# A macaron block with conv and gated linear attention: x by chunks at the head, the mixer's weights and its end in a new order

## The chip, the cores and the metric

One core of a Trainium2 chip runs one launch of the kernel. Its engines each work through a list of their own: TensorE (PE, with PEld for its weight loads), VectorE (DVE), ScalarE (ACT), GpSimd (POOL) and SyncE (SP), which here only issues transfers. The metric is the device time of the launch in microseconds (us), the median of the runs shown.

## The reference, cut to what matters

The input x has 512 rows of 1024 numbers (float32), and there is one layer:

```python
h = h + 1/2 * SwiGLU_1(RMSNorm(h))             # FFN1: 1024 -> 2 x 2816 -> 1024
u = RMSNorm(h); z = u @ W_in                   # mixer: conv value and gate, q, k, v, r, forget gate
y_conv = silu(LayerNorm(depthwise_conv31(GLU)))
y_gla  = rmsnorm_per_head(chunked gated linear attention) * silu(r)
h = h + concat([y_conv, y_gla]) @ W_out
h = h + 1/2 * SwiGLU_2(RMSNorm(h))             # FFN2
h = h + sigmoid(RMSNorm(h) @ W_g) * (p @ W_p)
out = RMSNorm(h)

def _swiglu(x, w_in, w_out):
    gate, up = jnp.split(x @ w_in, 2, axis=-1)
    return (jax.nn.silu(gate) * up) @ w_out
```

The norm of a row is a factor on that row, so a product can be started on x times the norm's gains, and the row's factor put on its result.

## The kernel before, in words

**Data and products.** Everything is kept transposed: features on the 128 partitions, the 512 rows along the free axis, so x is turned by TensorE (a product with the identity, `ident`) in eight chunks of 128 features, each with four 128x128 turns into one PSUM bank. Each factor of a product is cut in a high part of fewer bits (a cast, on ACT as a rule) and a low part, what the cast left (a subtraction, on DVE). A product of 128 features is then three matmuls of 512 columns: `mm3` does high by high, high weight by low x, low weight by high x. For x the parts are `hgH` and `hgL`; for weights `wr` is the raw tile, `wh` and `wl` its parts of 128x1024 (six of each), and `wa` parts of 128x512 in smaller buffers. There are two ways to make `wl`: the subtraction on DVE or POOL (`low`), or `added`, where ACT writes minus the rounded weight to it and a transfer issued by POOL adds the raw weight to that.

**The FFNs** use a scheme with fewer products: for most pairs of 256 of the 2816 features, seven products (units `m1` to `m7`) of half the rows (256 columns) on sums of weight and x blocks; the first two pairs, and those listed as `plain`, are computed plainly (units `h0` to `h7`). A list of units sets the order; before a unit runs, the parts of later units are prepared: a unit names jobs with a distance, and `AHEAD` is 4, so the cast of a unit's weights is put on ACT and DVE four units ahead (lines 580 to 600, 715 to 740). `hooks` puts other work after a named unit. The output product is done in parts over pairs (`second`, pieces named by their output column n and half g).

**The head** (lines 140 to 557) loads x in pieces by rows: four of 128x256 twice, and four of 128x512, and the weights of the first four output blocks between them (two gate, two up blocks of 128 features). The first two, `pg0` and `pu0`, use 128x4x128 pieces; `pg1` and `pu1` come after, each over all eight chunks of x (`zblock`). In the last of these, at chunk 7, `spread` puts the rows' norm factors over the partitions (four transposes). Squares of x, from which the norm comes, are summed by ACT, twelve instructions with an accumulator. SP issues the transfers in the order of the program.

**The end of FFN1 and the mixer.** `ahead` prepares the first weights of the mixer, four raw tiles of `in_w_in` with eight `wa` pairs, all from the hook of unit `m4` of pair 10. POOL makes their low parts. In the mixer, z's blocks for tokens (`tokblock`, four times, t = 0 to 3) are followed each by the gate `r` (ACT), the tokens' `y` times `r` (DVE, `y<-y,r`), and some of the convolution's taps (`taps(n)`, DVE instructions `cv<-glu,cw,cv`). Then TensorE turns `y`, ACT and DVE cut it in `ygH` and `ygL`, and the output product starts (`first_part(n)`, 12 matmuls for output block n on the attention's half, with weights `wo[n]`). The conv's LayerNorm runs beside it: `mub` collects the mean by products with the constant `mean` on the four conv blocks (the last two as one sum, `acc23`), `ln_sums` the squares, `ln_out` spreads the factor, and `yc` are the conv's outputs. These are put between matmuls of `first_part(3)` and `first_part(6)`.

Of the kernel before, what the change touches and what calls it, by code (L numbers as in the profile page):

```python
# [15 lines left out]
P = 128  # L16
# [46 lines left out]
def block_kernel(ctx: ExitStack, tc: tile.TileContext, a: dict, out: bass.AP):  # L63
# [75 lines left out]
    in_order(True)  # L139
    columns(vecs[:1], 8, "vcol1", nc.sync)()  # L140
    X_CUTS = (0, 2 * P, 4 * P, D)
    xt = [[] for _ in range(TB)]

    def load_x(i):

        c0, c1 = X_CUTS[i:i + 2]
        for t in range(TB):
            piece = bt(s="x")[:, 0:c1 - c0]
            nc.sync.dma_start(out=piece, in_=a["x"][0, t * P:(t + 1) * P, c0:c1])  # L149
            xt[t].append(piece)  # L150


# [57 lines left out]
    def parts(r3):  # L210

        return low(high(r3))
# [231 lines left out]
    hT = [big.tile([P, SEQ], F32, tag="H", bufs=DC, name=nm("h")) for _ in range(DC)]  # L444
    hg, xps = [], []

    def turn_x(c):
        ps = bank()
        for t in range(TB):
            i = min(c // 2, 2)  # L450
            c0 = c * P - X_CUTS[i]
            pe.transpose(ps[:, t * P:(t + 1) * P], xt[t][i][:, c0:c0 + P], ident)
        xps.append(ps)
# [3 lines left out]

    def take(ps, w, ks):

        for k in ks:  # L460
            mm3(ps, *rows_of(w, k), *hg[k], k == 0, k == DC - 1)

    ssx = tmp("ssx", 16, bufs=1)

    def square_x(i):
        for t in range(TB):
# [3 lines left out]
    def halves(c0):  # L470

        r3 = raw(DC, P)
        for k in range(0, DC, 4):
            def go(k=k):
                fetch(r3[:, k:k + 4], ffn1_in, k, 4, c0, P)
                return r3[:, k:k + 4]
            yield go

    def big4(r3):
        hi, lo = (bt(F32R, "wa").rearrange("p (k c) -> p k c", k=4) for _ in range(2))  # L480
        act.copy(hi, r3)
        return hi, lo, r3

    go_g, go_u = list(halves(0)), list(halves(DFF))
    load_x(0)
    raw_g = [go_g[0]()]
    load_x(1)
    raw_u = [go_u[0]()]
    raw_g.append(go_g[1]())
    load_x(2)  # L490
    raw_u.append(go_u[1]())
    turn_x(0)
    turn_x(1)
    pg0, pu0 = bank(), bank()
    split_x(0)
    wg0 = [low(big4(raw_g[0]))]
    split_x(1)
    take(pg0, wg0, (0,))
    turn_x(2)
    turn_x(3)  # L500
    split_x(2)
    take(pg0, wg0, (1,))
    split_x(3)
    wu0 = [low(big4(raw_u[0]))]
    take(pg0, wg0, (2, 3))
    act.copy(hT[0], xps[0])
    dve.tensor_copy(hT[1], xps[1])
    take(pu0, wu0, (0, 1))
    turn_x(4)
    take(pu0, wu0, (2, 3))  # L510
    wg0.append(low(big4(raw_g[1])))
    split_x(4)
    turn_x(5)
    split_x(5)
    act.copy(hT[2], xps[2])
    dve.tensor_copy(hT[3], xps[3])
    turn_x(6)
    take(pg0, wg0, (4,))
    split_x(6)
    turn_x(7)  # L520
    take(pg0, wg0, (5,))
    split_x(7)
    wu0.append(low(big4(raw_u[1])))
    raw_g1 = load(ffn1_in, 0, DC, P, P)
    raw_u1 = load(ffn1_in, 0, DC, DFF + P, P)
    take(pg0, wg0, (6, 7))
    take(pu0, wu0, range(4, DC))
    w1 = Left(ffn1_in, 2)
# [4 lines left out]
    for i in range(P // RANK):  # L533
        nc.sync.dma_start(out=made[2][i * RANK:(i + 1) * RANK, :], in_=a["gate_w_up"][0])
    square_x(0)
    early = [parts(raw_g1), parts(raw_u1)]
    for c in range(4, DC, 2):
        act.copy(hT[c], xps[c])
        dve.tensor_copy(hT[c + 1], xps[c + 1])
    square_x(1)  # L540
    square_x(2)
    ss = tmp("cs", 16)[:, :TB]
    dve.tensor_reduce(out=ss, in_=ssx.rearrange("p (t i) -> p t i", t=TB)[:, :, 0:3],
                      axis=mybir.AxisListType.X, op=ALU.add)
    mid = [rsqrt_mean(ss, D, TB, between=lambda: w1.part("a11"))]
    pg1 = zblock(early[0], hg)
    pu1 = zblock(early[1], hg, {2: lambda: w1.part("a12"), 7: lambda: mid.append(spread(mid[0]))})
    xb = Right(hg, "ffn1_norm")


# [51 lines left out]
    def ffn(w_in, w_out, x, gname, given, first, rsb, hooks, plain):  # L602
# [10 lines left out]
        def row(i):  # L613
            return rsb[:, i * HALF:(i + 1) * HALF].unsqueeze(1).to_broadcast([P, 2, HALF])

# [16 lines left out]
        def scaled(ps, name):  # L632
            o = tmp(name)
            dve.tensor_tensor(out=o, in0=ps, in1=rsb, op=ALU.mult)
            return o
# [106 lines left out]

        def second(cut):
# [53 lines left out]
            if not last:  # L797
                return [piece(n, 0, True, True, ("g2", f0) if n == 0 else None) for n in range(0, DC, 2)]
            return ([piece(n, 0, True, False) for n in range(0, 6, 2)],
                    [piece(n, 1, False, True) for n in range(0, 6, 2)] + [piece(6, 0, True, False),  # L800
# [11 lines left out]
        for i in plain:  # L812
            for j in range(8):
                add(f"h{j}", i)
                if j % 2:
# [25 lines left out]
        p0 = pairs[0]  # L841
        for i in range(2):
            s = silu(scaled(first[i][0], "g1"))
            gated_block(p0, s, scaled(first[i][1], "u1"), i)
        more = hooks.get(("h0", 1), lambda *_: None)
        hooks["h0", 1] = lambda *_: (act_parts(p0), more())
        drive(units)
# [12 lines left out]
    hooks = sums_hooks(xb, ("t2", "t3", "t1", "t4"), (("h7", 1), ("h2", 2), ("h5", 2), ("m1", 3)))  # L860
    hooks.update({("h%d" % (i + 1), 1): f for i, f in enumerate(xb.steps())})
    hooks.update({("m5", 3): lambda *_: made[0](), ("m5", 4): lambda *_: constants(),
                  ("m4", 10): lambda *_: w_ahead.extend([ahead(w_in, D_CONV, 2 * P), ahead(w_in, 0, 2 * P)])})
    rsb = mid[1]
    hg, norm = ffn(ffn1_in, a["ffn1_w_out"][0], xb, "mix_norm", {0: Left(ffn1_in, 0), 1: w1},
                   ((pg0, pu0), (pg1, pu1)), rsb, hooks, (1, 2))
    pool.on = False
# [356 lines left out]
    def part(ps, w, ks, first, last, mid={}):  # L1224
        for k in ks:
            if k in mid:
                mid[k]()
            mm3(ps, *rows_of(w, k), *mix[k], first and k == ks[0], last and k == ks[-1])

# [7 lines left out]
    for t in range(TB):  # L1237
# [20 lines left out]
        if t == 1:  # L1258
            oload(2)
            ytok = []  # L1260
            for i in range(TB):
# [18 lines left out]
    pe.matmul(mub, mean, acc[1], start=False, stop=False)  # L1280
    taps(2)
    for h in range(4):
# [58 lines left out]

    first_part(3, wo[3], {4: ln_sums})
    first_part(6, wo[6], {5: ln_out})

# [189 lines left out]
```

## Time and profile before

| | |
|---|---|
| median of 3 runs | 959.59 us (959.04 to 960.14) |
| the profiled execution | 959.53 us, its span 957.8 us |
| TensorE busy in the span | 941.6 us (98%), 5790 matmuls and turns |
| DVE, ACT, POOL busy | 732.2, 450.3 and 49.7 us |
| mean granted TensorE clock | 0.997 |

The span is the time from the first to the last recorded work; 1.73 us of the execution lie around it. Instruction names read out<-in, so `ps<-hgH,wh` is a matmul into a PSUM bank from the high parts of x and weights; all instructions carry line L46, that of a helper which records the order, so the names tell them apart. Since TensorE is busy for 98%, the question of every edit is which of its few idle times, or which slow stretch, it touches.

### The profile page before, as it was taken

The numbers are of one execution on the slowest core, as the hardware profiler recorded it, in microseconds if no ns is written. First come the engines' busy times: TensorE is split into PE (matmuls) and PEld (weight loads), VectorE is DVE, ScalarE is ACT, GpSimd is POOL, SyncE is SP. The second block draws the span as 40 slices with busy tenths as digits, with TensorE's granted clock in tenths as the row PEclk, the third lists the DMA queues.
The fourth block names the chain that finished last, engine by engine and source line by source line (L and its number), as shares of the span: only waits on it lengthen the run. The fifth ranks groups of instructions, "written<-read, shape, count | busy, mean of one in ns | idle before, by whom it ended". The sixth has DMA issues, their size and how long they took to land.

```text
span 957.8 us, 14314 instructions
## 1 busy us (share of the span) xinstructions
PE 941.6 (98%) x5790; PEld 835.6 (87%) x5790; DVE 732.2 (76%) x979; ACT 450.3 (47%) x694; POOL 49.7 (5%) x59
## 2 busy tenths in 40 slices
PE   7999999999999999999999999999999999999996
PEld 5888999999999978888878889999999999998885
DVE  4685888887788585999995749787878778867554
ACT  5753443434443463473564855444334443346442
POOL 0000200000000210101030010000000000000000
PEclk9999999999999999999999999999999999999998
DMA  7632323342323471337553571432244233334102
GB/s 223 184 111 66 97 81 108 113 133 74 104 89 110 142 188 45 88 89 175 118 112 104 153 176 44 132 110 67 91 129 121 74 102 102 111 111 154 44 1 88
DMA packets 105510, 104.49 MB, mean 109 GB/s; under 512 B 4756, under 2 KB 96582, under 8 KB 105445
## 3 DMA queue, kind: packets, MB, share of 16 engines
q1 hardware_dynamic: 102708, 94.67, 32.1%
q0 software_dynamic: 2736, 8.91, 5.3%
q8 instruction: 45, 0.74, 0.3%
q14 instruction: 21, 0.16, 0.1%
HBM read 92.56 MB, written 2.10 MB: 99 GB/s over the span
## 4 chain that ended last, share of the span: by engine, by line
PE 92%; issue 2%; DVE 2%; DMA 2%; ACT 1%; POOL 1%; SPq 0%; POOLq 0%; DVEq 0%; ACTq 0%
PE ps L46 91%; DMA wr<-in_w_in 1%; PE ax L46 1%; DVE cv L46 1%; ACT wh L46 0%; DMA wr<-in_ffn_w_in 0%; POOL rs L46 0%; DVE y L46 0%; DVE wl L46 0%; ACT wl L46 0%; ACT wa L46 0%; POOL wa L46 0%; SPq L149 0%; DVE rs L46 0%; DVE g L46 0%
## 5 line engine op out<-in xcount | busy, mean ns | idle before, releaser
L46 DVE TENSOR_TENSOR wl<-wr,wh 128x1024 fp32r<-128x1024 f32 (+1 forms) x168 | 199.7, 1201 | 47.4 <-ACT wh L46 46.9
L46 PE MATMUL ps<-hgH,wh 128*128 128x256 f32 (+1 forms) x752 | 235.3, 313 | 0.0
L46 PE MATMUL ps<-hgH,wl 128*128 128x256 f32 (+1 forms) x752 | 234.9, 312 | 0.0
L46 PE MATMUL ps<-hgL,wh 128*128 128x256 f32 (+1 forms) x752 | 234.9, 312 | 0.0
L46 ACT CAST wh<-wr 128x1024 fp32r<-128x1024 f32 (+1 forms) x183 | 185.0, 1026 | 33.8 <-PE ps L46 23.1
L46 PEld LDWEIGHTS ps<-hgL,wh 128*128 128x128 f32 x752 | 143.4, 191 | 8.8
L46 PEld LDWEIGHTS ps<-hgH,wh 128*128 128x128 f32 x752 | 143.4, 191 | 8.7
L46 PEld LDWEIGHTS ps<-hgH,wl 128*128 128x128 f32 x752 | 143.4, 191 | 8.2
L46 PE MATMUL ps<-actH,wh 128*128 128x512 f32 x352 | 137.6, 391 | 1.2 <-ACT actH L46 1.2
L46 PE MATMUL ps<-actL,wh 128*128 128x512 f32 x352 | 137.5, 391 | 0.2 <-DVE actL L46 0.2
L46 PE MATMUL ps<-actH,wl 128*128 128x512 f32 x352 | 137.0, 389 | 0.0
L46 ACT ACTIVATE s<-g 128x512 f32<-128x512 f32 x48 | 30.4, 632 | 187.6 <-DVE g L46 187.6
L46 DVE SCALAR_TENSOR_TENSOR cv<-glu,cw,cv 128x502 f32<-128x502 f32 (+24 forms) x120 | 82.1, 741 | 0.6
L46 PEld LDWEIGHTS ps<-actH,wh 128*128 128x128 f32 x352 | 66.2, 188 | 14.4 <-ACT actH L46 1.6
L46 PEld LDWEIGHTS ps<-actH,wl 128*128 128x128 f32 x352 | 66.1, 188 | 13.9
L46 PEld LDWEIGHTS ps<-actL,wh 128*128 128x128 f32 x352 | 66.2, 188 | 13.1 <-DVE actL L46 0.5
L46 DVE SCALAR_TENSOR_TENSOR h<-ps,h 128x512 f32<-128x512 f32 x80 | 54.4, 688 | 22.1 <-PE ps L46 22.1
L46 ACT COPY sq<-ps 128x512 f32<-128x512 f32 x34 | 19.9, 585 | 73.8 <-PE ps L46 73.8
L46 PE MATMUL ps<-wh,hgH 128*128 128x512 f32 (+1 forms) x136 | 52.4, 385 | 0.0
L46 PE MATMUL ps<-wl,hgH 128*128 128x512 f32 (+1 forms) x136 | 51.7, 380 | 0.0
L46 PE MATMUL ps<-wh,hgL 128*128 128x512 f32 (+1 forms) x136 | 51.3, 377 | 0.0
L46 ACT CAST actH<-m 128x512 fp32r<-128x512 f32 x44 | 25.4, 618 | 39.2 <-DVE m L46 39.2
(230 smaller groups left out, 1656.9 us busy)
## 6 DMA issues: line engine op xcount, KB each, us to landing
wr<-in_ffn_w_in SPq DMA_DIRECT2D x86, 512.0 KB
wr<-in_ffn_w_out SPq DMA_DIRECT2D x32, 512.0 KB
wr<-in_w_in SPq DMA_DIRECT2D x20, 512.0 KB
wl<-wr POOLq DMA_DIRECT2D x15, 512.0 KB, 5.0
wr<-in_ffn_w_out SPq DMA_DIRECT2D x16, 384.0 KB
wr<-in_w_out SPq DMA_DIRECT2D x8, 512.0 KB
wr<-in_ple_w_gate SPq DMA_DIRECT2D x8, 512.0 KB
out<-y SPq DMA_DIRECT2D x8, 256.0 KB
```

What stands on the lines that cost most here:

```text
L46: inst = call(*args, **kwargs)
```

## The change

The diff has four groups. The first is the **head**: the first chunk of x (all rows, 128 columns) is the first transfer of SP, the first norm's gains move to ACT's queue, x comes by column chunks and weights by rows of one or two chunks (for all four blocks), and the four blocks are accumulated together, chunk after chunk, 12 matmuls each. `warm_up` adds 14 turns of the identity whose result isn't used. Squares are whole tiles on ACT with a reduction on DVE, and `spread` and the first pairs' gates (`first_out`) move behind unit `h0`. Two steps of FFN1's block sums (`xb.steps()`) come earlier, and later ones at other units. The second is **`ahead`**: low parts by `added`, and its second call after piece n = 4 of the last output part, `("last", 4)`. The third is the distance of `m5`'s cast, `AHEAD + 1` in each pair rather than in the first alone. The fourth is the **mixer's end**: order of the three matmuls, of taps, casts and LayerNorm steps.

```diff
     in_order(True)
-    columns(vecs[:1], 8, "vcol1", nc.sync)()
-    X_CUTS = (0, 2 * P, 4 * P, D)
...
+    def warm_up(n):
+        idle = aux()
+        for _ in range(n):
+            pe.transpose(idle[:, 0:P], ident, ident)
+
+    warm_up(10)
+    turn_vec = columns(vecs[:1], 8, "vcol1", nc.scalar)
...
-        return [[low(w, pool) for w in high4(load(src, 0, DC, c, P))] for c in range(c0, c0 + ncol, P)]
+        return [[added(w) for w in high4(load(src, 0, DC, c, P))] for c in range(c0, c0 + ncol, P)]
...
+    def load_x(c, n):
+        nt = TB // n
+        for h in range(n):
+            tile_ = bt(s="x").rearrange("p (t c) -> p t c", t=nt)
+            nc.sync.dma_start(out=tile_, in_=a["x"][0, h * nt * P:(h + 1) * nt * P, c * P:(c + n) * P]
+                              .rearrange("(t p) c -> p t c", p=P))
...
     def square_x(i):
-        for t in range(TB):
-            junk = tmp("sq", bufs=3)[:, 0:X_CUTS[i + 1] - X_CUTS[i]]
-            act.activation(junk, xt[t][i], AF.Square, accum_out=ssx[:, 4 * t + i:4 * t + i + 1])
...
+        act.activation(sq, tile_, AF.Square)
...
+        dve.tensor_reduce(out=sums[-1][:, t0:t0 + nt], in_=sq, axis=mybir.AxisListType.X, op=ALU.add)
...
+    def take(k, between):
+        wh, wl = (t[:, k % 2] for t in wpart[k // 2])
+        xh, xl = hg[k]
+        for i, (w, x) in enumerate(((wh, xh), (wl, xh), (wh, xl))):
+            for b in range(4):
+                c0 = (b // 2 + 2 * (b % 2)) * P
+                pe.matmul(ps0[b], w[:, c0:c0 + P], x, start=(k == i == 0), stop=(k == DC - 1 and i == 2))
+            if i == 1:
+                between()
+
+    for c in range(2):
+        load_x(c, 1)
+        load_w(c, 1)
+    load_x(2, 2)
+    load_w(2, 1)
+    load_w(3, 1)
+    for c in (4, 6):
+        load_x(c, 2)
+        load_w(c, 2)
...
+    turn_vec()
+    turn_x(0)
+    warm_up(4)
+    ps0 = [bank() for _ in range(4)]
+    split_w(0, 1, dve.tensor_copy)
+    split_x(0)
...
+    for c in range(DC):
+        nxt = {0: (1,), 1: (2, 3), 3: (4, 5), 5: (6, 7)}.get(c, ())
+        take(c, lambda: [turn_x(n) for n in nxt])
+        if c < 3:
+            split_w(c + 1, 1)
+        elif c in (3, 5):
+            split_w(c + 1, 2)
+        for n in nxt:
+            split_x(n)
+        keep_x(c)
...
-            before = [(AHEAD + (kind == 'm5' and i == start), lambda: p.part(part))] if part else []
+            before = [(AHEAD + (kind == 'm5'), lambda: p.part(part))] if part else []
...
-                  ("m4", 10): lambda *_: w_ahead.extend([ahead(w_in, D_CONV, 2 * P), ahead(w_in, 0, 2 * P)])})
+                  ("m4", 10): lambda *_: w_ahead.append(ahead(w_in, D_CONV, 2 * P)),
+                  ("last", 4): lambda *_: w_ahead.append(ahead(w_in, 0, 2 * P))})
...
+            wo[4] = [added(w) for w in ohigh(4)]
...
-        if t > 1:
-            wo[t + 2] = [added(w) for w in ohigh(t + 2)]
+        if t == 2:
+            wo[5] = [added(w) for w in ohigh(5)]
         if t > 0:
-            taps((0, 2, 5, 5)[t])
+            taps((0, 2, 5, 2)[t])
...
-    taps(2)
+    taps(1)
...
-    pe.matmul(mub, mean, acc23, start=False, stop=True)
-    first_part(5, wo[5])
+    first_part(5, wo[5], {6: lambda: pe.matmul(mub, mean, acc23, start=False, stop=True)})
...
-    first_part(3, wo[3], {4: ln_sums})
-    first_part(6, wo[6], {5: ln_out})
+    first_part(3, wo[3], {6: ln_sums})
+    first_part(6, wo[6], {6: ln_out})
```

At **the head, on SP**, the transfers before were these (`x` four pieces of rows, `wr` weights of one block):

```order
L122 DMA vcol1r<-in_ffn_norm 8x128
L149 DMA x_98<-in_x 128x256
L149 DMA x_100<-in_x 128x256
L149 DMA x_102<-in_x 128x256
L149 DMA x_104<-in_x 128x256
L181 DMA wr_96<-in_ffn_w_in 128x4x128
L149 DMA x_107<-in_x 128x256
```

And now, with `x` all rows of one chunk, and `wr` one chunk's rows for two gate and two up blocks:

```order
L447 DMA x_108<-in_x 128x4x128
L482 DMA wr_104<-in_ffn_w_in 128x256 x2
L447 DMA x_112<-in_x 128x4x128
L482 DMA wr_104<-in_ffn_w_in 128x256 x2
L447 DMA x_116<-in_x 128x2x256
L447 DMA x_118<-in_x 128x2x256
L482 DMA wr_105<-in_ffn_w_in 128x256 x4
```

The first weights moved from the sixth transfer to the second and third. On TensorE, now, at the same place:

```order
L46 MATMUL ax_81<-ident 128x128 x10
L46 MATMUL ax_161<-ident,vcol1r 128x8
L46 MATMUL ps_164<-ident,x_108 128x128 x4
L46 MATMUL ax_169<-ident 128x128 x4
L46 MATMUL ps_174<-hgH_182,wh_178 128x512
L46 MATMUL ps_175<-hgH_182,wh_178 128x512
L46 MATMUL ps_176<-hgH_182,wh_178 128x512
L46 MATMUL ps_177<-hgH_182,wh_178 128x512
```

Four blocks (`ps_174` to `ps_177`) now take chunk 0 after four turns of x; before, eight turns stood ahead of the first block's first matmul.

At **the end of FFN1, on ACT**, before (`wa` the mixer's weights, `wh` FFN1's last output weights, `actH` the last features):

```order
L46 CAST wa_3347<-wr_3345 128x512
L46 CAST wa_3350<-wr_3345 128x512
L46 CAST wa_3357<-wr_3355 128x512
L46 CAST wa_3360<-wr_3355 128x512
L46 CAST wh_3367<-wr_3229 128x768
L46 ACTIVATE s_3397<-g_588_3395 128x512
L46 CAST wh_3399<-wr_3264 128x768
L46 CAST actH_3424<-m_3323 128x512
```

And now:

```order
L46 ACTIVATE wa_3350<-wr_3347 128x512
L46 ACTIVATE wa_3353<-wr_3347 128x512
L46 CAST wh_3361<-wr_3239 128x768
L46 ACTIVATE s_3391<-g_568_3389 128x512
L46 CAST wh_3393<-wr_3274 128x768
L46 CAST actH_3418<-m_3333 128x512
L46 CAST actH_3422<-m_3333 128x512
L46 CAST wh_3426<-wr_3300 128x768
L46 CAST wa_3452<-wr_3450 128x512
L46 CAST wa_3455<-wr_3450 128x512
```

The third and fourth raw tiles of the mixer moved behind `actH`; `ACTIVATE wa` is the negated copy of `added`.

At **the mixer's end, on DVE**, before (`y` the last token block, `ygL` the first low parts for the output product):

```order
L46 SCALAR_TENSOR_TENSOR cv_3617<-glu_4035,cw,cv_3617 128x502
L46 SCALAR_TENSOR_TENSOR cv_3617<-glu_4035,cw,cv_3617 128x503
L46 SCALAR_TENSOR_TENSOR cv_3617<-glu_4035,cw,cv_3617 128x504
L46 SCALAR_TENSOR_TENSOR cv_3617<-glu_4035,cw,cv_3617 128x505
L46 TENSOR_TENSOR y_4725<-y_4725,r_4802 128x512
L46 SCALAR_TENSOR_TENSOR cv_3617<-glu_4035,cw,cv_3617 128x506
L46 SCALAR_TENSOR_TENSOR cv_3617<-glu_4035,cw,cv_3617 128x507
L46 SCALAR_TENSOR_TENSOR ygL_4846<-ps_4819,vcol,ygH_4844 128x512
```

And now:

```order
L46 TENSOR_TENSOR y_4748<-y_4748,r_4786 128x512
L46 SCALAR_TENSOR_TENSOR cv_3635<-glu_4053,cw,cv_3635 128x502
L46 TENSOR_TENSOR y_4753<-y_4753,r_4830 128x512
L46 SCALAR_TENSOR_TENSOR cv_3635<-glu_4053,cw,cv_3635 128x503
L46 SCALAR_TENSOR_TENSOR ygL_4860<-ps_4834,vcol,ygH_4858 128x512
```

Three taps that stood ahead of the last `y` and one that stood between it and `ygL` moved behind the four `ygL`.

More of the change, by code (lines that the diff above doesn't have):

```diff
@@ L470, in halves @@
[L470 to L488, printed above, removed]
@@ L511, in block_kernel @@
[L511 to L527, printed above, removed]
+        tile_, t0, nt = squares[i]
+        sq = tmp("sq", bufs=3).rearrange("p (t c) -> p t c", t=nt)
@@ L534, in block_kernel, with rows_x @@
         nc.sync.dma_start(out=made[2][i * RANK:(i + 1) * RANK, :], in_=a["gate_w_up"][0])
[L535 to L547, printed above, removed]
+    turn_vec()
[4 more added lines that the diff above has]
+    split_x(0)
+    mid = []
+    def rows_x():
+        ss = tmp("cs", 16)[:, :TB]
+        dve.tensor_reduce(out=ss, in_=ssx[:, 0:4 * len(sums)].rearrange("p (i t) -> p t i", t=TB),
+                          axis=mybir.AxisListType.X, op=ALU.add)
+        mid.append(rsqrt_mean(ss, D, TB, between=lambda: w1.part("a11")))
+    for c in range(DC):
[8 more added lines that the diff above has]
+        keep_x(c)
+        for i in {1: (0, 1), 2: (2,), 3: (3, 4), 4: (5,), 5: (6, 7)}.get(c, ()):
+            square_x(i)
+        if c == 6:
+            rows_x()
+            w1.part("a12")
     xb = Right(hg, "ffn1_norm")
+    steps = xb.steps()
+    steps[0]()
+    steps[1]()
     def constants():
@@ L841, in ffn, with first_out @@
         p0 = pairs[0]
-        for i in range(2):
-            s = silu(scaled(first[i][0], "g1"))
-            gated_block(p0, s, scaled(first[i][1], "u1"), i)
+        def first_out(norm_of_rows):
+            got["rsb"] = norm_of_rows
+            for i in range(2):
+                s = silu(scaled(first[i][0], "g1"))
+                gated_block(p0, s, scaled(first[i][1], "u1"), i)
+        late = callable(rsb)
+        if not late:
+            first_out(rsb)
         more = hooks.get(("h0", 1), lambda *_: None)
-        hooks["h0", 1] = lambda *_: (act_parts(p0), more())
+        hooks["h0", 1] = lambda *_: (first_out(rsb()) if late else None, act_parts(p0), more())
         drive(units)
@@ L1227, in part @@
                 mid[k]()
-            mm3(ps, *rows_of(w, k), *mix[k], first and k == ks[0], last and k == ks[-1])
+            (wh, wl), (xh, xl) = rows_of(w, k), mix[k]
+            pe.matmul(ps, wh, xh, start=(first and k == ks[0]), stop=False)
+            pe.matmul(ps, wl, xh, start=False, stop=False)
+            pe.matmul(ps, wh, xl, start=False, stop=(last and k == ks[-1]))
     def first_part(n, w, mid={}):
```

77 lines of the change are left out of this document (32 added, 45 removed).

## The prediction

> **What bounds the kernel now.** I read the page's busy times first, then the windows by stage, then TensorE's (PE's) waits, and last the timeline around each wait.
>
> ```profile
> PE 941.6 (98%) x5790; PEld 835.6 (87%) x5790; DVE 732.2 (76%) x979; ACT 450.3 (47%) x694; POOL 49.7 (5%) x59
> ```
>
> ```profile
> 0.00:36.00 36.00, 30.87 (x139) 24.12 (x140) 16.53 (x28) 21.04 (x48) 1.95 (x10) 1.00 0.73 212
> 36.00:339.00 303.00, 303.00 (x1971) 278.15 (x1970) 237.78 (x280) 134.01 (x184) 15.30 (x14) 1.00 0.34 106
> 339.00:346.00 7.00, 5.60 (x24) 4.09 (x23) 4.89 (x7) 4.92 (x7) 0.92 (x1) 1.00 0.89 237
> 490.00:498.00 8.00, 6.06 (x31) 3.91 (x30) 7.86 (x12) 7.18 (x14) 3.56 (x4) 1.00 0.74 120
> ```
>
> ```profile
> PE ps L46 <- DVE y L46: 1.6, 1, 1.6
> PE ps L46 <- ACT wa L46: 1.6, 1, 1.6
> ```
>
> A window's second column is PE's busy time. From 36 to 339 us it fills the window, so a cast or transfer that comes earlier there gains nothing. PE is idle at the head (5.1 us of 36), at the end of the first FFN (1.4 of 7) and at the mixer's end (1.9 of 8); two have their row among the waits, the third's is below, and the change edits all three places. The forecast is therefore a sum of three small terms.
>
> **The head.** The rows are SP's first x transfers, the identity ready, the first turn of x, the first weights' cast, the first matmul, eight turns early and eight late, and the end of the four blocks with `spread` in it.
>
> ```profile
> 1.26 1.78 SPq L149 DMA_DIRECT2D x<-in_x  x4
> 2.30 0.17 PEld L46 LDWEIGHTS ax<-ident,vcol1r 8*128 8x128 f32 x1 [2.30 <-POOL ident masks.py:199]
> ...
> 3.34 1.02 PE L46 MATMUL ps<-ident,x 128*128 128x128 f32 x2 [0.77 <-DMA x<-in_x]
> ...
> 7.27 0.62 ACT L46 CAST wa<-wr 128x512 fp32r<-128x512 f32 x1 [1.02 <-DMA wr<-in_ffn_w_in]
> ...
> 7.94 0.80 PE L46 MATMUL ps<-hgH,wa 128*128 128x512 f32 x1 [1.56 <-ACT wa L46]
> ...
> 9.39 1.78 PE L46 MATMUL ps<-ident,x 128*128 128x128 f32 x8
> ```
>
> ```profile
> 16.53 1.04 PE L46 MATMUL ps<-ident,x 128*128 128x128 f32 x8
> 17.32 0.47 PE L46 MATMUL ps<-hgH,wa 128*128 128x512 f32 x1
> ...
> 34.15 1.05 PE L46 MATMUL ax<-ident,rs 128*128 128x128 f32 x8
> ...
> 35.28 0.39 PE L46 MATMUL ps<-hgL,wh 128*128 128x512 f32 x1
> 35.51 0.39 PE L46 MATMUL ps<-hgH,wl 128*128 128x512 f32 x1
> ```
>
> At full rate a matmul of 512 columns starts every 0.23 us (35.28 to 35.51; 3.86 / 17 = 0.227 over the rows of the next part), a turn costs 0.1 (16.53 to 17.32, eight) and `spread` with the longer start after it 0.9 (34.15 to 35.28, less 0.23). The four blocks end at 35.51 + 0.23 = 35.74. They are 96 matmuls before and after. What sets their start is the weights: the first raw piece is there at 7.27, 6.0 us after SP's first x issue, since five transfers stand ahead of it.
>
> Afterwards PE starts with ten identity turns at about 2.3. Early turns cost 0.22 each (1.78 / 8), so they end at 4.5, and the norm's column after them at 4.7. The first chunk of x is SP's first transfer: by the first x pieces (2.1 us from issue 1.26 to the turn at 3.34) it lands near 3.0, with twice the bytes by estimate at 3.4 to 4.3; the chunk is hidden behind the added turns. Four turns (0.9) and ACT's `hgH` behind them (0.7 by estimate, as a cast of that size takes 0.62) give a first matmul near 6.3. The weights' cast, now on DVE and as long, must start by 5.6; at 0.45 an issue (1.78 / 4) both pieces are issued by about 2.1, behind x alone.
>
> From there: 96 x 0.227 = 21.8, 28 turns x 0.11 = 3.1, changes between turns and matmuls 0.5, slow start 0.6, and `spread`, which now lies in the next unit, 0.9. That is 26.9, end at 33.2, a gain of 35.74 - 33.2 = **2.6**. The 0.6 is half-rate work until about 7.5: before, PE is slow to about 10.9, with idle time between 3.3 and 7.9; now it is nearly without pause from 2.3. Bounds: start at 5.9 and never slow, 3.7 gained; weights landing late, start at 6.7, slow to 10.9 (2.1 lost) 0.7. I take 2.6, nearer the good end, since both delays of before (weights sixth, PE idle) are what is moved. Squares, reductions and later transfers lie beside PE: a chunk is 12 x 0.227 + 0.4 = 3.1 us of PE and 512 KB, 169 GB/s where the first window moves 212. Without that cover, a chunk's transfer that comes late stops all four blocks.
>
> The granted clock column reads 1.00 even where the eight turns take 1.78, so durations decide here. The Trainium skill (TensorE: Matmul & The Clock Gate, What's actually happening) says that the array starts at half rate and is released after a busy window of about 3.4 us that runs freely. This case agrees in the ratio 1.78 to 0.8, and by that page alone, as an estimate, busy from 2.3 would release it between 5.7 and 9.1, the sum being 952.6 to 954.0.
>
> **The first FFN's end.** PE's last matmuls before the stall and after, then ACT, POOL's subtractions, the accumulations' time to landing elsewhere in the program, and DVE:
>
> ```profile
> 337.63 0.39 PE L46 MATMUL ps<-actH,wh 128*128 128x512 f32 x1
> ...
> 341.49 0.39 PE L46 MATMUL ps<-actH,wl 128*128 128x512 f32 x1
> 343.06 0.51 PE L46 MATMUL ps<-actH,wh 128*128 128x512 f32 x1 [1.18 <-ACT actH L46]
> ...
> 344.12 0.40 PE L46 MATMUL ps<-actH,wl 128*128 128x512 f32 x1
> ```
>
> ```profile
> 329.90 1.14 ACT L46 CAST wa<-wr 128x512 fp32r<-128x512 f32 x2 [2.66 <-DMA wr<-in_w_in]
> ...
> 335.16 1.14 ACT L46 CAST wa<-wr 128x512 fp32r<-128x512 f32 x2 [0.56 <-DMA wr<-in_w_in]
> 336.21 0.83 ACT L46 CAST wh<-wr 128x768 fp32r<-128x768 f32 x1
> ```
>
> ```profile
> 334.16 5.76 POOL L46 TENSOR_TENSOR wa<-wr,wa 128x512 fp32r<-128x512 f32 x4 [0.57 <-ACT wa L46]
> ```
>
> ```profile
> wl<-wr POOLq DMA_DIRECT2D x15, 512.0 KB, 5.0
> ```
>
> ```profile
> 337.07 1.69 DVE L46 TENSOR_TENSOR wl<-wr,wh 128x768 fp32r<-128x768 f32 x1 [2.93 <-ACT wh L46]
> ...
> 341.66 0.69 DVE L46 TENSOR_TENSOR m<-u,s 128x512 f32<-128x512 f32 x1
> ```
>
> The stall is 344.12 - 341.49 - 3 x 0.227 = 1.95 over three matmuls, 1.34 of it ahead of the first. ACT's queue holds the last output weights (`wh` at 336.21) behind four mixer tiles, of which the last landed at 335.16. Now only two stand ahead; the second landed at 329.90, with two casts and two negated copies done by 332.2. The way from `wh` at 336.21 to `m`'s end at 342.35 is 6.1 us; the same from 332.2 ends at 338.3, and `actH` 0.6 later, against PE's need at 341.72. So the stall goes whole, with 2.8 us to spare: **-1.95**. What is late next are the two moved tiles. POOL issues their accumulations, which hold a raw tile some 5 us (the median of 5.0 above) where POOL's subtraction took 1.4 (5.76 / 4); they are due in the mixer some 25 us later, so I take zero; bounds -1.95 and, half of the stall coming back there, -1.0.
>
> The Trainium skill (SBUF — State Buffer, SBUF: two separate sides) warns that a transfer issued by GpSimd waits for its descriptors while some DVE instructions hold a shared port. The page's median of 5.0 beside a DVE that is busy for 76% holds that already; if it doubled, the sum would not move.
>
> **The mixer's end.** DVE, ACT, and PE:
>
> ```profile
> 490.50 3.07 DVE L46 SCALAR_TENSOR_TENSOR cv<-glu,cw,cv 128x502 f32<-128x502 f32 x4
> 493.49 0.68 DVE L46 TENSOR_TENSOR y<-y,r 128x512 f32<-128x512 f32 x1
> ```
>
> ```profile
> 490.89 0.81 ACT L46 ACTIVATE r<-ps,rs 128x512 f32<-128x512 f32 x1
> ...
> 494.59 2.42 ACT L46 ACTIVATE ygH<-ps,vcol 128x512 fp32r<-128x512 f32 x4 [0.82 <-PE ps L46]
> ```
>
> ```profile
> 494.23 0.66 PE L46 MATMUL ps<-ident,y 128*128 128x128 f32 x4 [1.59 <-DVE y L46]
> ...
> 496.32 0.50 PE L46 MATMUL ps<-ygL,wh 128*128 128x512 f32 x1 [0.35 <-DVE ygL L46]
> ...
> 504.43 1.02 PE L46 MATMUL ax<-acc,mean 128*128 128x512 f32 x2
> ```
>
> ```profile
> 515.10 1.05 PE L46 MATMUL ax<-ident,rs 128*128 128x128 f32 x8
> 515.91 0.48 PE L46 MATMUL ps<-ygH,wh 128*128 128x512 f32 x1
> ```
>
> ```profile
> 516.97 0.82 ACT L46 ACTIVATE ycH<-yc,vcol 128x512 fp32r<-128x512 f32 x1 [6.44 <-DVE yc L46]
> ```
>
> The last `r` is done at 491.70, but `y` waits behind four taps until 493.49. With the taps behind it `y` ends at 492.4, PE's turns start at 492.5 instead of 494.23, `ygH` ends at 493.5 and `ygL` 0.7 later. Since the low part of x now comes third, PE has two matmuls before it needs `ygL` at 494.25: the output product runs as if begun at 493.8, against 496.32 - 0.23 = 496.1. Gain 2.3. Then the LayerNorm may give some back. Eight taps (0.77 each, 3.07 / 4) behind `ygL` end near 502.4 and `acc23` at 503.1; PE asks for it six matmuls later than before, at 504.43 - 2.3 + 1.4 = 503.5. After `spread` only six matmuls cover the way to `ycH` where nine did: from PE's next matmul (515.91) `ycH` took 1.9 us to 517.8, six cover 1.4, so 0.4 is lost, and 0.15 at its low part. Net **-1.75**; bounds -2.4 (no loss) and -0.7 (`acc23` late by the 0.75 of one more tap and `ycH` by 0.9).
>
> **The distance of `m5`'s cast** counts zero: ACT is 47% busy and PE doesn't wait for its casts between 36 and 339.
>
> The sum: 959.53 - 2.6 - 1.95 - 1.75 = 953.2; the profiled execution is 0.06 under the median, so nothing is added.
>
> **The rivals.**
>
> *The head's gain is mostly lost* (weights land late in 512-byte pieces, or PE stays slow to 10.9): gain 0.7 instead of 2.6, **955.1**. For it: the first window's transfers are already the busiest of the program (212 GB/s). Against: 512 KB ahead of the first matmul instead of 768. Chance 0.17.
>
> *The LayerNorm's chain takes the mixer's gain*: DVE, 7.86 busy of 8 there, gives `acc23` and `yc` late and PE waits at both; gain 0 instead of 1.75, **955.0**. For it: margins of 0.4. Chance 0.18.
>
> *Casts one unit earlier make PE wait.*
>
> ```profile
> L46 ACT CAST wh<-wr 128x1024 fp32r<-128x1024 f32 (+1 forms) x183 | 185.0, 1026 | 33.8 <-PE ps L46 23.1
> ```
>
> `wh` has six tiles; ACT already idles 23.1 us for PE to release one. In 15 places of the two FFNs the cast of `s1` now comes before another; if the one behind it comes late by its 1.03 us each time, that is +15.4, so **968.6**; it decides from 6.3 / 15 = 0.42 us each. Against: PE's 303 of 303, and no wait for `wh` among PE's. Chance 0.06.
>
> *The accumulations hold raw tiles*, and the mixer's first products wait for their weights by 2 to 4 us: about **956**. Chance 0.06.
>
> **How the numbers follow.** The forecast has 0.5; its own range is 952 to 954.5. What is left, 0.03, is more gain than its bounds. A measurement of this kernel can tell about 0.2% (1.9 us) from no change. Faster than that is the forecast, nearly all of the first two rivals and the fourth: 0.88; both terms failing together, or an unknown of 2 us: same 0.06; slower, the third: 0.06. The range leaves out the cast rival and the best bounds: 951.2 to 956.6.
>
> **What would show it.** Head: the first `hgH,wh` matmul near 6.3, `spread` about 2.6 earlier. FFN: no PE wait for `actH`. Mixer: turns of `y` at PE without a wait of over 0.6, a short wait for `ycH`. It is wrong if the first matmul comes after 7.5, if `wh` appears among PE's waits, or if PE idles in 346 to 380.

## The result

The changed kernel takes 954.35 us, median of four runs (953.21 to 955.30), against 959.32 for the kernel before in the same set (958.90 to 960.14): a ratio of 0.9943, 95% interval 0.9929 to 0.9958. Timed a second time beside other kernels it took 952.81 (five runs, 952.68 to 954.59; ratio 0.9934, interval 0.9921 to 0.9946). The forecast was 953.2, range 951.2 to 956.6, so it holds in both sets. The profiled execution took 953.21 with a span of 951.1 (before 957.8). Runs of the changed kernel differ by up to 2.1 us in one set, those of the kernel before by 1.2 here and by 1.7 in a longer set (26 runs, 959.06 to 960.77). That has to be understood before the terms can be compared.

### The profile after

The windows of the changed kernel by stage (second column: TensorE's busy time), with the same borders as in the prediction. The stages of the changed kernel come up to 6.5 us earlier, so a window holds slightly other work:

```profile
0.00:36.00 36.00, 34.31 (x168) 28.63 (x169) 23.66 (x39) 23.12 (x40) 2.79 (x10) 1.00 0.77 236
36.00:339.00 303.00, 303.00 (x1970) 278.16 (x1969) 237.46 (x283) 135.09 (x184) 9.31 (x12) 1.00 0.36 107
339.00:346.00 7.00, 7.00 (x32) 5.82 (x31) 3.39 (x5) 6.34 (x10) 2.87 (x4) 1.00 1.14 258
490.00:498.00 8.00, 8.00 (x37) 6.60 (x36) 7.72 (x11) 3.06 (x4) 0.86 (x1) 1.00 0.80 203
```

And all of TensorE's waits:

```profile
PE ax L46 <- POOL ident masks.py:199: 1.6, 1, 1.6
PE ps L46 <- ACT ycH L46: 0.2, 1, 0.2
```

The waits for `y`, for the first weights and for `actH` have left the list; the short one for `ycH` is the one that was forecast. The head's idle time fell from 5.1 to 1.7 us, nearly all of it the wait for the identity.

**The head.** TensorE's first rows:

```profile
1.61 2.40 PE L46 MATMUL ax<-ident 128*128 128x128 f32 x10 [1.61 <-POOL ident masks.py:199]
...
4.27 1.11 PE L46 MATMUL ps<-ident,x 128*128 128x128 f32 x4
...
5.17 1.06 PE L46 MATMUL ax<-ident 128*128 128x128 f32 x4
...
6.25 1.19 PE L46 MATMUL ps<-hgH,wh 128*128 128x512 f32 x4
...
7.29 1.08 PE L46 MATMUL ps<-hgH,wl 128*128 128x512 f32 x4
```

The two casts that this first matmul needs, of x on ACT and of the weights on DVE:

```profile
5.42 0.69 ACT L46 ACTIVATE hgH<-ps,vcol 128x512 fp32r<-128x512 f32 x1 [2.49 <-PE ps L46]
```

```profile
5.68 0.43 DVE L46 CAST wh<-wr 128x512 fp32r<-128x512 f32 x1 [1.14 <-DMA wr<-in_ffn_w_in]
```

The first matmul on data starts at 6.25 (before 7.94, forecast 6.3). Both casts end at 6.11, so the weights' landing and the turns of x hold it alike. The four matmuls from 6.25 to 7.29 start 0.26 apart, near the full rate's 0.227, while before even the turns at 9.39 started 0.21 apart, which is the low rate.

**The first FFN's end**, DVE and ACT:

```profile
329.14 0.82 ACT L46 CAST wh<-wr 128x768 fp32r<-128x768 f32 x1
```

```profile
329.99 0.96 DVE L46 TENSOR_TENSOR wl<-wr,wh 128x768 fp32r<-128x768 f32 x1 [1.07 <-ACT wh L46]
...
333.85 0.69 DVE L46 TENSOR_TENSOR m<-u,s 128x512 f32<-128x512 f32 x1
```

From `wh` to the end of `m` is 334.54 - 329.14 = 5.4 us, where it was 6.1, and `m` is done 7.8 us earlier than before (342.35), 3.4 of it by the head. TensorE doesn't pause there. The `wl` behind this `wh` takes 0.96 in place of 1.69: that one ran beside POOL's subtraction before, and POOL does none now. The Trainium skill (SBUF — State Buffer, SBUF: two separate sides) gives a rule for that: DVE and GpSimd share one port pair, and when a DVE instruction with two SBUF inputs meets a GpSimd instruction that reads SBUF, the one that starts first blocks the other. The numbers agree, 1.69 beside POOL and 0.96 without.

**The mixer's end**, TensorE:

```profile
487.45 0.65 PE L46 MATMUL ps<-ident,y 128*128 128x128 f32 x4
...
510.63 0.40 PE L46 MATMUL ps<-ygL,wh 128*128 128x512 f32 x1
511.26 0.50 PE L46 MATMUL ps<-ycH,wh 128*128 128x512 f32 x1 [0.23 <-ACT ycH L46]
```

The turns of the last `y` no longer wait, and the new pause before `ycH` is 0.63 - 0.23 = 0.40 us.

### Where the time went

The same instructions of both profiles, set against each other, give the gain up to each place:

| place (start of) | before | after | gain so far |
|---|---|---|---|
| first matmul on data | 7.94 | 6.25 | 1.69 |
| first 256-column matmul (behind all of the head) | 101.04 | 97.65 | 3.39 |
| last `actH` matmul of the first FFN | 363.19 | 357.82 | 5.37 |
| first 256-column matmul of the second FFN | 588.06 | 581.53 | 6.53 |
| span | 957.8 | 951.1 | 6.7 |

By terms: head 3.39 (forecast 2.6), first FFN's end 1.98 (1.95), mixer 1.16 (1.75).

### The profile page after: what moved, and what is told of

Its sections match the earlier page's. It is cut to its first block, busy times and chain, and to the rows that moved or that the text cites. A ratio compares the mean times of both kernels' runs of the same rounds, so it can differ in the third digit from the quotient of the medians.

```text
span 951.1 us, 14343 instructions
## 1 busy us (share of the span) xinstructions
PE 941.6 (99%) x5804; PEld 837.1 (88%) x5804; DVE 734.9 (77%) x988; ACT 452.0 (48%) x685; POOL 46.4 (5%) x59
## 4 chain that ended last, share of the span: by engine, by line
PE 99%; DVE 0%; ACT 0%; issue 0%; POOL 0%; POOLq 0%; DVEq 0%; ACTq 0%
PE ps L46 97%; PE ax L46 2%; ACT ycH L46 0%; DVE yc L46 0%; POOLq L1546 0%; DVE y L46 0%; ACT s L46 0%; DVEq L1546 0%; DVE s L46 0%; DVE g L46 0%; ACT sq L46 0%; DVE rs L46 0%; POOL ident masks.py:199 0%; DVE ms L46 0%; POOL mean L46 0%
## 5 line engine op out<-in xcount | busy, mean ns | idle before, releaser
L46 DVE TENSOR_TENSOR wl<-wr,wh 128x1024 fp32r<-128x1024 f32 (+2 forms) x172 | 201.7, 1184 | 48.0 <-ACT wh L46 47.7
L46 PE MATMUL ps<-hgH,wh 128*128 128x256 f32 (+1 forms) x768 | 237.9, 315 | 0.0
L46 PE MATMUL ps<-hgL,wh 128*128 128x256 f32 (+1 forms) x768 | 237.6, 314 | 0.0
L46 PE MATMUL ps<-hgH,wl 128*128 128x256 f32 (+1 forms) x768 | 237.3, 314 | 0.0
L46 ACT CAST wh<-wr 128x1024 fp32r<-128x1024 f32 (+2 forms) x186 | 187.0, 1021 | 36.7 <-PE ps L46 26.5
L46 PEld LDWEIGHTS ps<-hgH,wh 128*128 128x128 f32 x768 | 146.3, 191 | 10.0 <-ACT hgH L46 0.7
L46 PEld LDWEIGHTS ps<-hgH,wl 128*128 128x128 f32 x768 | 146.4, 191 | 8.9
L46 PEld LDWEIGHTS ps<-hgL,wh 128*128 128x128 f32 x768 | 146.1, 191 | 9.0
```

What stands on the lines that cost most here:

```text
L46: inst = call(*args, **kwargs)
```

## The experiments

### The groups one by one

The first four kernels are the kernel before with one group of the change each. The head alone:

```diff
-    columns(vecs[:1], 8, "vcol1", nc.sync)()
+    warm_up(10)
+    turn_vec = columns(vecs[:1], 8, "vcol1", nc.scalar)
...
+    for c in range(2):
+        load_x(c, 1)
+        load_w(c, 1)
...
+        take(c, lambda: [turn_x(n) for n in nxt])
```

> The kernel before with the head's group alone. Theory (three separate terms): the first real matmul at about 6.25 us instead of 7.94, and everything behind the four blocks earlier by 3.4 us if TensorE runs at full rate from the first matmul, by about 1.7 if it gets its full rate one stretch of 3.4 us later; time 956 to 958. The four timed runs of the changed kernel lie in two pairs (953.2 and 953.5, 955.2 and 955.3), so both may show here. Rival (a pair's difference has another cause, behind the head): the head's shift is 3.4 in each profile, and the runs of this kernel lie close together near 956.

Measured: 957.43 (six runs: 956.02, 956.12, 956.79, 958.06, 958.14, 958.36) against 959.76, ratio 0.9972, interval 0.9961 to 0.9984. Its profile is of a run at 956.79:

```profile
6.24 2.02 PE L46 MATMUL ps<-hgH,wh 128*128 128x512 f32 x4
8.09 1.10 PE L46 MATMUL ps<-hgH,wl 128*128 128x512 f32 x4
```

The first matmul starts where it did in the changed kernel, but its group of four takes 2.02 instead of 1.19: the low rate lasts to 8.1, and the first 256-column matmul starts at 98.47 instead of 97.65. So the theory holds for this profile, and the rival, a cause behind the head alone, doesn't explain it: 0.82 us differ before anything else has run.

The first FFN's end alone:

```diff
-        return [[low(w, pool) for w in high4(load(src, 0, DC, c, P))] for c in range(c0, c0 + ncol, P)]
+        return [[added(w) for w in high4(load(src, 0, DC, c, P))] for c in range(c0, c0 + ncol, P)]
...
-                  ("m4", 10): lambda *_: w_ahead.extend([ahead(w_in, D_CONV, 2 * P), ahead(w_in, 0, 2 * P)])})
+                  ("m4", 10): lambda *_: w_ahead.append(ahead(w_in, D_CONV, 2 * P)),
+                  ("last", 4): lambda *_: w_ahead.append(ahead(w_in, 0, 2 * P))})
```

> The kernel before with the mixer's low parts by accumulation and the second call moved, nothing else. Theory: TensorE's wait for actH at 341 us is gone, -1.95, less 0.2 at the first norm of the mixer: 957.6, and this in each run. Rival (the raw tiles are held and the mixer starts late): the 1.95 come back as waits between 346 and 380, time 959 or more.

Measured: 957.45 (957.14 to 958.49), ratio 0.9975, interval 0.9965 to 0.9985. From the first 256-column matmul to the last `actH` one it takes 260.17 us, as the changed kernel does (260.17), and the kernel before 262.15: 1.98, and from there to the second FFN nothing comes back (224.84 against 224.87). The rival falls.

The mixer's end alone:

```diff
-            mm3(ps, *rows_of(w, k), *mix[k], first and k == ks[0], last and k == ks[-1])
+            (wh, wl), (xh, xl) = rows_of(w, k), mix[k]
+            pe.matmul(ps, wh, xh, start=(first and k == ks[0]), stop=False)
+            pe.matmul(ps, wl, xh, start=False, stop=False)
+            pe.matmul(ps, wh, xl, start=False, stop=(last and k == ks[-1]))
...
-            taps((0, 2, 5, 5)[t])
+            taps((0, 2, 5, 2)[t])
...
-    taps(2)
+    taps(1)
...
-    first_part(3, wo[3], {4: ln_sums})
-    first_part(6, wo[6], {5: ln_out})
+    first_part(3, wo[3], {6: ln_sums})
+    first_part(6, wo[6], {6: ln_out})
```

> The kernel before with the mixer's end alone. Theory: TensorE's waits for y and ygL (2.8 us in all) go down to about 0.9, the wait for ycH takes 0.4 and one in the second FFN's first units 0.2: net -1.4 to -1.6, time 957.8 to 958.0. Rival (the LayerNorm's chain sets the end): the gain ends below 0.5, time 958.9 or more.

Measured: 957.83 (957.60 to 958.96), ratio 0.9982, interval 0.9973 to 0.9990. From the last `actH` matmul to the second FFN: 223.33 against 224.87, a gain of 1.54. Between the same pairs of instructions, 1.76 goes at the wait for `y` and 0.5 at the first `ygL`; 0.1 comes back right behind that, 0.41 before `ycH`, and 0.2 at the two steps that follow it. The rival (all given back) falls.

The distance of `m5`'s cast alone:

```diff
-            before = [(AHEAD + (kind == 'm5' and i == start), lambda: p.part(part))] if part else []
+            before = [(AHEAD + (kind == 'm5'), lambda: p.part(part))] if part else []
```

> The kernel before with the distance of m5's cast alone. Theory: no change, 959.3, since TensorE does not wait for casts there. Rival (one more wh tile held): waits for wh among TensorE's waits, 0.4 us or more at 15 places, time above 961.

Measured: 959.89 (959.17 to 960.58), ratio 1.0001, interval 0.9992 to 1.0009, and no wait for `wh` appears among TensorE's. It does nothing that can be measured, and the rival of one more `wh` tile held falls.

The four medians' differences are -2.33, -2.31, -1.93 and +0.13, -6.4 together; the changed kernel's two medians lie 5.0 and 6.8 under the kernel before. The terms add up within the runs' spread.

### When TensorE gets its full rate

> The changed kernel once more, as the yardstick of this call and for a second profile. Theory: a median near 954.3 with runs from 953.2 to 955.3, whose places differ only at the head: the profile shows all of the 1.95 at the first FFN's end and 1.4 to 1.6 at the mixer's, and full rate from 5.0 to 8.4 us, 953.2 + half of what it comes later than 6.2. Rival: part of the 2 us between runs lies behind the head.

The changed kernel again, without an edit: 952.81 (952.68, 952.71, 952.81, 953.64, 954.59). Its profile, of a run at 952.71:

```profile
1.61 2.39 PE L46 MATMUL ax<-ident 128*128 128x128 f32 x10 [1.61 <-POOL ident masks.py:199]
...
5.17 0.63 PE L46 MATMUL ax<-ident 128*128 128x128 f32 x4
6.25 1.17 PE L46 MATMUL ps<-hgH,wh 128*128 128x512 f32 x4 [0.45 <-DVE wh L46]
```

Here the four identity turns at 5.17 take 0.63 instead of 1.06: the full rate came within them. The first 256-column matmul starts at 97.61, and the mixer's stretch takes 223.25 (gain 1.62). The first profile's 1.16 was thus low for another reason: 0.3 of it lies at 362 to 365, where three starts came some 0.1 late each; nothing shows what they waited for, and it isn't in this profile.

The changed kernel without its identity turns:

```diff
-    warm_up(10)
     turn_vec = columns(vecs[:1], 8, "vcol1", nc.scalar)
...
     turn_x(0)
-    warm_up(4)
```

> The changed kernel without its 14 identity turns. In the profiles so far TensorE comes to full rate 3.0 to 6.5 us after its work became continuous (10.9 to 13.8 in four profiles of the old head, where it does so near 7.7; 6.2 and 8.1 with the new head, near 1.6). Theory: without the turns it becomes continuous near 3.8, so full rate comes near 7 to 10.5; the first real matmul stays near 6.1, and the median is 0.8 to 1.2 us above the changed kernel's. Rival (the turns only fill time, the rate comes by itself): the same median within 0.3.

Measured: 955.54 (954.55 to 955.57), ratio 0.9955, interval 0.9943 to 0.9968; 2.7 above the median of the changed kernel that was timed beside it, and 2.1 above the median of all nine runs of the changed kernel (953.47). Either is about twice what I expected or more, since without the turns TensorE also pauses between the turns of x and the first matmul:

```profile
3.75 1.12 PE L46 MATMUL ps<-ident,x 128*128 128x128 f32 x4 [1.16 <-DMA x<-in_x]
6.50 2.05 PE L46 MATMUL ps<-hgH,wh 128*128 128x512 f32 x4 [1.63 <-DVE wh L46]
8.35 1.91 PE L46 MATMUL ps<-hgH,wl 128*128 128x512 f32 x4
10.05 1.05 PE L46 MATMUL ps<-ident,x 128*128 128x128 f32 x4
```

The low rate goes on to 12.1. The turns do more than fill time: the rival falls.

A pause at the start:

```diff
-    warm_up(10)
+    warm_up(3)
```

> The changed kernel with three identity turns instead of ten at the start, so that TensorE pauses for about 1.2 us until the first chunk of x has landed, and then goes on; the first real matmul stays at 6.1 to 6.3. Theory (only work without a pause counts): full rate comes 3.4 to 6.8 after 3.8, so 7.2 to 10.6, and the median is 0.7 to 1.3 above the changed kernel's 952.8 to 954.3. Rival (the start of the first work counts, pause or not): full rate at 5 to 8.4 and the same median.

Measured: 955.17 (954.56 to 955.60), ratio 0.9953, interval 0.9940 to 0.9965. The first matmul starts at 6.00, earlier than with ten turns, and the kernel is slower all the same:

```profile
1.61 0.90 PE L46 MATMUL ax<-ident 128*128 128x128 f32 x3 [1.61 <-POOL ident masks.py:199]
2.57 0.27 PE L46 MATMUL ax<-ident,vcol1r 8*128 8x8 f32 x1
3.74 1.11 PE L46 MATMUL ps<-ident,x 128*128 128x128 f32 x4 [0.90 <-DMA x<-in_x]
...
6.00 2.05 PE L46 MATMUL ps<-hgH,wh 128*128 128x512 f32 x4 [0.29 <-DVE wh L46]
```

A pause of 0.9 us at 2.8 was followed by full rate only at 10.4, 6.7 after the work went on, where the rival had 5 to 8.4. In this profile the start of the first work alone doesn't count.

Work without a pause (one run, 955.94):

```diff
-    warm_up(10)
+    warm_up(40)
```

> The changed kernel with 40 identity turns instead of 10 at the start, for a look at when full rate comes in work without a pause: each turn starts 0.21 us after the last at the low rate, 0.11 at the full. Theory: between 5.0 and 8.4 (3.4 to 6.8 after the start at 1.61), and the first real matmul near 8.5 to 10, the time 2 to 3 us above the changed kernel's. Rival (the rate follows the real matmuls or their columns, not the array's work): no change of rate before the first real matmul.

```profile
1.61 6.07 PE L46 MATMUL ax<-ident 128*128 128x128 f32 x40 [1.61 <-POOL ident masks.py:199]
```

Turn by turn, the starts lie 0.21 apart up to 4.65 and 0.11 apart from 4.79: full rate 3.1 us after the start, by identity turns alone. That is earlier than the 3.4 I set as the least, and no matmul on data has run by then, so the rival of this kernel falls.

The old head with identity turns alone:

```diff
+    warm_up(5)
     columns(vecs[:1], 8, "vcol1", nc.sync)()
...
     turn_x(0)
     turn_x(1)
+    warm_up(8)
     pg0, pu0 = bank(), bank()
```

> The kernel before with identity turns alone: five ahead of the norm's column and eight where TensorE waited for the first weights (6.0 to 7.9); loads and matmuls in the old order. Theory (the rate is part of the head's gain): full rate comes at 5.5 to 9 instead of 10.9 to 13.8, the first real matmul stays near 7.7 to 8.0, and the gain is about half of the 3 to 4 us of low rate that go, 1.4 to 2: 957.7. Rival (the order of the loads makes the whole gain): no change, 959.5.

Measured: 959.10 (eleven runs, 958.76 to 960.96) against 959.65, ratio 0.9996, interval 0.9987 to 1.0005: no difference that can be told, so the theory's 1.4 to 2 isn't there and by the times its rival, no change, holds. The rate did come early, at about 8.3:

```profile
7.84 0.67 PE L46 MATMUL ps<-hgH,wa 128*128 128x512 f32 x1
8.35 0.39 PE L46 MATMUL ps<-hgL,wa 128*128 128x512 f32 x1
8.57 0.39 PE L46 MATMUL ps<-hgH,wa 128*128 128x512 f32 x1
8.80 1.03 PE L46 MATMUL ps<-ident,x 128*128 128x128 f32 x8
...
10.96 0.50 PE L46 MATMUL ps<-hgL,wa 128*128 128x512 f32 x1 [0.20 <-DVE hgL L46]
```

but the old order can't use it. The eight turns that took 1.78 take 1.03, and then TensorE waits for `hgL` and, at 13.8, 0.5 for a piece of x. This profile's first 256-column matmul starts at 100.49, the other old heads' at 101.04 to 101.98, the new head's with full rate at 97.61 to 97.67. So the turns alone are worth 0.5 to 1.5 in the old order (in profiles; the times don't separate them). With the full rate at like times, 8.3 here and 8.1 in the head alone, the new order is worth 2.0 more (100.49 for 98.47), 1.6 of it the earlier first matmul (6.24 for 7.84).

All profiles so far; "without a pause" is where the work begins that has no pause of over 0.6 us in it until the full rate comes. The trace settles that last time: besides the instructions it keeps a list of the clock that TensorE was granted, and the list's first entry, full rate, begins at the time in the third column. There the starts of turns and matmuls double their pace:

| kernel | without a pause from | full rate from | first 256-column matmul |
|---|---|---|---|
| before | 7.9 | 10.9 | 101.04 |
| mixer's end alone | 7.6 | 12.9 | 101.51 |
| `m5` alone | 7.6 | 13.2 | 101.64 |
| first FFN's end alone | 7.8 | 13.8 | 101.98 |
| changed kernel | 1.6 | 6.3 | 97.65 |
| the same again | 1.6 | 5.2 | 97.61 |
| head alone | 1.6 | 8.1 | 98.47 |
| ten turns cut to three | 3.7 | 10.4 | 99.50 |
| no identity turns | 6.5 | 12.1 | 100.39 |
| ten turns made forty | 1.6 | 4.7 | 100.76 |
| old head with turns | 1.6 | 8.3 | 100.49 |

With the new head, each microsecond of low rate behind the first matmul costs about half, when the 0.25 by which the first matmul starts earlier or later is taken out: (99.50 - 97.65 + 0.25) / (10.4 - 6.0) = 0.48, (100.39 - 97.65 - 0.25) / (12.1 - 6.5) = 0.44. The changed kernel, the yardstick of both, has no low rate to speak of there. In all profiles, those of the next part included, the full rate comes 3.0 to 6.7 us after the pauses end, another time in each execution. Profiles of one head differ by it: 97.61 to 98.47 with the new head and all its turns, 101.04 to 101.98 with the old one, 0.9 each. By estimate, half of the whole width, it is up to 1.9. That it explains all of the spread between runs isn't shown, since only one run of each set has a profile. The Trainium skill (TensorE: Matmul & The Clock Gate, What's actually happening) describes a gate that halves the rate until the array was busy for a whole window of some 3.4 us, with windows that run freely. By it, as an estimate, the wait would lie between 3.4 and 6.8 us; the runs' 3.0 to 6.7 agree in the width and begin a little lower. The list of granted clocks agrees too: the stretch at full rate lasts 938.7, 942.1 or 945.5 us in the 13 profiles, which is 275, 276 and 277 times 3.413. The granted clock column of the profile stays at 1.00 in all of these rows, because it takes the time ahead of the list's first entry as full.

### Two tries at a faster kernel

The LayerNorm's spread one step earlier:

```diff
-    first_part(6, wo[6], {6: ln_out})
+    first_part(6, wo[6], {5: ln_out})
```

> The changed kernel with the spread of the LayerNorm's factor at k = 5 of first_part(6), as before the change, and the sums at k = 6 as now. The changed kernel's profile has the factor ready at 507.97 and the spread would stand at 507.9, so TensorE would not wait there, and nine matmuls cover the way to ycH. Theory: the 0.41 us before the first ycH matmul go, -0.4 (953.9 against 954.3). Rival (the conv's outputs after the first become the wait): the next yc are late instead and the change is below 0.1.

Measured: 952.80 (952.46 to 954.32), ratio 0.9930, interval 0.9918 to 0.9943, beside 952.81 for the changed kernel. The wait before `ycH` is gone, and a smaller one stands before the spread:

```profile
507.30 0.40 PE L46 MATMUL ps<-ygL,wh 128*128 128x512 f32 x1
507.76 1.13 PE L46 MATMUL ax<-ident,rs 128*128 128x128 f32 x8
```

0.46 - 0.23 = 0.23 of waiting for 0.40: by the profiles 222.93 for that stretch against 223.25, and the lowest run 0.2 lower. The theory named the right wait but not the new one; the times can't tell the two kernels apart.

With it, the first chunk of x on ACT's queue:

```diff
-    act.copy(warm, ones)
...
-    warm_up(10)
+    x0 = bt(s="x").rearrange("p (t c) -> p t c", t=TB)
+    nc.scalar.dma_start(out=x0, in_=a["x"][0, :, 0:P].rearrange("(t p) c -> p t c", p=P))
     turn_vec = columns(vecs[:1], 8, "vcol1", nc.scalar)
+    act.copy(warm, ones)
+    warm_up(8)
```

> As the run before it, and the first chunk of x is issued by ACT (ahead of the norm's gains and the table load), so that SP's first transfers are the first weights; eight identity turns instead of ten ahead of the first chunk. Theory: the first weights, which landed at 4.1 and 5.6, land by 5.0, x at about 3.9, and the first real matmul comes at 5.8 instead of 6.25: -0.4 more, if full rate is not put off by the two turns that are left out. Rival (both come at the rate of the same engines): the first matmul stays at 6.2.

Measured: 953.78 (953.64 to 954.57), ratio 0.9938, interval 0.9925 to 0.9952: slower than the one before it by 1.0 by the medians.

```profile
1.61 1.97 PE L46 MATMUL ax<-ident 128*128 128x128 f32 x8 [1.61 <-POOL ident masks.py:199]
4.36 0.24 PE L46 MATMUL ax<-ident,vcol1r 8*128 8x8 f32 x1 [0.78 <-DMA vcol1r<-in_ffn_norm]
4.53 1.11 PE L46 MATMUL ps<-ident,x 128*128 128x128 f32 x4
...
6.42 2.08 PE L46 MATMUL ps<-hgH,wh 128*128 128x512 f32 x4
```

The norm's gains, 4 KB, now issue behind x on ACT's queue and hold TensorE up to 4.36. So the turns of x come later, not earlier, and the pause of 0.8 put the full rate off to 10.0. Neither theory nor rival had that: I had watched the two transfers that were moved and not the third, which they moved past.

## Why the prediction was right, and where its terms were off

**The sum.** 953.2 was forecast; the two medians are 954.35 and 952.81. All three terms have the forecast sign and place, and the groups alone confirm each. Three slips in the sum's bounds move nothing: a start at 5.9 and no slow start give 3.6 and not 3.7, the mixer without loss 2.3 and not 2.4, and the best bounds together 951.5, which the range from 951.2 on doesn't leave out.

**The head (forecast 2.6, bounds 0.7 to 3.7).** First matmul: 6.3 forecast, 6.25 measured; x landed in time behind the added turns. That the number is so close is in part luck. The wait until 2.30 was read as the identity's, but TensorE's list of waits puts it on the norm's gains; the identity's last instruction on POOL ends at 1.56, and the turns started at 1.61. The 0.7 that this frees is spent again: the ten turns and the four of x took 0.5 longer than was entered, and the rest lies between the cast's end and the first matmul. The weights' cast, which was to start by 5.6, starts at 5.68 and ends with x's at 6.11; in the second profile TensorE's last wait there, 0.45, is for it. The chunk by chunk stretch ran without a starved chunk. The step that was mis-sized is the slow start. (The ratio 1.78 to 0.8 set a row's length against a distance of starts; by starts the turns go from 0.21 to 0.11.) "Half-rate work until about 7.5" was entered as one number, and "PE is slow to about 10.9" taken from one profile as a property of the kernel before. Both are draws: the new head's full rate came at 5.2 to 8.1 in three profiles, the old one's at 10.9 to 13.8 in four. In the profile of the changed kernel it came with the first matmul: the four blocks end at 31.44 and with `spread`'s 0.9 at 32.3, where 33.2 was forecast. Of that difference, 0.6 is the slow start and some 0.2 the turns and changes, which took less than was entered. Hence 3.39 in the profiled pair, 2.57 (101.04 to 98.47) in the head alone, 2.33 by its median. The forecast's mechanism, that less pausing gives the full rate earlier, is what the pause and no-turns kernels show; what it lacked was how much of the head's gain depends on it. Without the turns 2.1 to 2.7 us of the changed kernel's gain were gone, and of the 3.39 in the profiled pair 0.65 was left (101.04 to 100.39). One sign that was named didn't show: `spread` starts at 34.16, as before (34.15), since it moved behind 12 more matmuls, a shift that the sum had and the sign had not.

**The first FFN's end (1.95).** 1.98 in both profiles. "The moved tiles come late" was costed at zero, and nothing came back between 346 and 380 in the kernel with this group alone. The chain was shorter than I had taken (5.4 for 6.1), since DVE no longer ran beside POOL's subtraction; it was not needed.

**The mixer's end (1.75).** 1.54 alone, 1.16 and 1.62 in the two profiles of the changed kernel. The wait for `y` gave 1.76, not 1.96: 0.20 of that step is the start of turns behind the matmul with `mean`, and stays. The wait for `ycH`, forecast at 0.4, measured 0.40, and the steps behind it 0.2, where 0.15 was entered. The asked-for margin at `acc23` held: it was ready at 498.1 and asked for at 498.6.

**The rivals.** Casts one unit earlier: 959.89, no effect. Their sign, `wh` among TensorE's waits, does appear in the second profile, but at the head's first matmul (0.45 at 6.25) and not in the FFNs. The LayerNorm's chain took 0.6 in all, not 1.75. Held raw tiles: no wait. The head's rival, "PE stays slow to 10.9", is what the same head does with a pause at the start (10.4), at a price of 1.9 at the first 256-column matmul; with all its turns the changed kernel had the full rate by 6.3 in both of its profiles.

## What to carry to other kernels

At a kernel's start, two things set the first stretch: when the first operands are there, and since when TensorE has worked without a pause. They have to be changed together: filler in the old order gained 0.5 us that the times can't separate, the new order without filler lost 2.1 to 2.7 of its gain. When a stage's baseline comes from one profile and the stage has a random part, take it as a range: look at the same rows in each profile that shares the stage. And before a transfer is moved to another queue, list the small ones that it then stands ahead of.

## What was not expected of the hardware

The rate of TensorE doubled (0.21 to 0.11 us a turn) on identity turns alone, 3.1 us after their start, while the profile's clock column reads 1.00; the trace's list of granted clocks has the step, at 4.70. After a pause of 0.8 to 0.9 us in the first five microseconds the full rate came 5.7 to 6.7 us later, at 10 us of the program rather than at 5 to 8. One profile each with such a pause (10.0 and 10.4) doesn't show how short a pause may be; after one of 0.47 in the old head with turns it came at 8.3.
